# An encoder trunk on one core: the first strips fetched in another order, squares summed on GpSimd, and eight idle products in a LayerNorm

## The chip, the cores and the metric

The kernel runs on one core of a Trainium2 chip. A core has five engines that run side by side and meet at semaphores: TensorE (products; the profile's PE, and PEld for its weight loads), VectorE (DVE), ScalarE (ACT), GpSimd (POOL) and SyncE (SP), whose queue issues nearly all the transfers here. TensorE writes its results to PSUM; operands lie in SBUF. The metric is the device time of one execution in microseconds, as the median of several runs. Beside the runs there is one profiled execution, and its trace is what is read here.

## The reference

Two layers over 512 tokens of width 1024, all in float32. Each sub-layer is `x = x + RMSNorm(f(RMSNorm(x)))`.

```python
for i in range(DEPTH):                      # DEPTH = 2
    g = sandwich_gains[i]
    h = rms_norm(x, g[0])
    m = parallel_conv_mla(h, ...) if i % 2 == 0 else conformer_conv(h, ...)
    x = x + rms_norm(m, g[1])
    h = rms_norm(x, g[2])
    x = x + rms_norm(squared_relu_mlp(h, mlp_w1[i], mlp_w2[i]), g[3])

def conformer_conv(h, w_pw1, b_pw1, w_dw, b_dw, ln_g, ln_b, w_pw2, b_pw2):
    u = h @ w_pw1 + b_pw1
    a, g = jnp.split(u, 2, axis=-1)
    u = depthwise_conv(a * jax.nn.sigmoid(g), w_dw) + b_dw
    u = jax.nn.silu(layer_norm(u, ln_g, ln_b))
    return u @ w_pw2 + b_pw2
```

Layer 0 has a short gated convolution and eight heads of latent attention with one input projection (`w_in`); layer 1 has the Conformer module above. Each layer ends with an MLP of hidden width 4096.

## The kernel before

**Layout.** Activations lie with channels on the 128 partitions and tokens along the free axis: eight tiles of 128 channels (`NC` = 8). A float32 product is made as three products of rounded parts. Every operand is split into a high half (`hi`, the value rounded to the product's input type) and a low half (`lo`, the rest); `mm` (L239) issues high by high (L243), high weight by low activation (L244), low weight by high activation (L245).

**Strips.** Weights come in strips of 128 output columns, 128x1024 elements, 512 KB. `strip` (L207) issues the DMA into `raw` (two buffers at the start), lets ScalarE write `whi` (L220) and GpSimd write `wlo = raw - whi` (L221). With `cuts` it does this in pieces of columns, each piece with a DMA, an ACT and a POOL instruction. A strip's column piece k is the weight for channel tile k.

**The start.** Inside a block with the order of TensorE, VectorE and ScalarE written out by hand (L574), products go through `bit(i, k)` (L584): strip i of the input projection with channel tile k of x, three products of 512 columns (L590 to L592). `busy(n)` (L578) issues n products with a tile of zeros that nobody reads. `scale_x(j)` (L598) fetches x tile j, multiplies it by the gain on VectorE (L601) and writes its high half on ScalarE (L602); `rest_x(j)` (L605) writes the low half on VectorE (L607). `square_x` and `add_x` (L611, L615) make the sum of squares for the first RMSNorm, whose sum over channels is a product with a column of ones (L365, in `Sum.done`). Strips 0 and 1 are walked through side by side, then strip 2, then strip 3. The order of SP's and GpSimd's instructions is left to a planner that simulates the program when it is built.

**Two halves.** From the first layer's output projection on, the tokens are worked in halves A and B, so that one half's products cover the other's norms. The list `M2` names the steps of the last phase in order: `up`, `down` (MLP), `pw1`, `pw2` (Conformer), `join` (residual and next norm), `norm` (the LayerNorm). A `join` or `norm` is a chain that TensorE can't feed itself; while it is written out, `pace` and `hold` (L300, L307) pull the other half's next steps in, as many as stand in the list before this half's next one. In `M2` only VectorE's order is the written one; TensorE's, ScalarE's, GpSimd's and SP's are the planner's.

**The sums.** `Sum.square` (L345) squares a tile on ScalarE (L355) into PSUM and puts the addition on a list, which VectorE does at the next `settle` (L330); `done` sums over channels on TensorE (L365); `rstd` (L381) is a chain of twelve small VectorE instructions (L388 to L416); `spread` (L426) puts the result on all partitions with two or three small products (L430). `rstds` (L374) is these three in a row. `layer_norm` (L900) of a half subtracts the mean (L914), sums the squares, multiplies by the root (L922), applies gain, bias and silu (L925) and splits the result into `h` (L227, L230), which `pw2` reads.

**The gain row.** `gtok` holds the last norm's gain on all partitions, for the end of half B, where tokens lie on the partitions. It has a place of its own from the beginning, and its DMA is written at L1030, in the first `turn` step near the end.

Of the kernel before, what the change touches and what calls it, by code (L numbers as in the profile page):

```python
# [9 lines left out]
F32 = mybir.dt.float32  # L10
# [6 lines left out]
P = 128  # L17
T = 512
# [109 lines left out]
def trunk(ctx: ExitStack, tc: tile.TileContext, a, out: bass.AP, out_b: bass.AP):  # L128
# [23 lines left out]
    def tmp(kind, dt=F32):  # L152
        if kind in CHAIN:
            return new(ap, kind, CHAIN[kind], HW, dt)
        tag, bufs, w = scope["tags"][kind]
        return new(scope["sb"], tag, bufs, w, dt)
# [35 lines left out]

    kst = cp.tile([P, NK], F32, name="kst")
    vec = cp.tile([P, NV], F32, name="vec")
    gtok = cp.tile([P, D], F32, name="gtok")
    ident = kst[:, K_ID : K_ID + P]
    sel = kst[:, K_SEL : K_SEL + P]
    one = kst[:, K_ONE : K_ONE + 1]
# [5 lines left out]
        nc.sync.dma_start(t.t, a["xT"][j * P : (j + 1) * P, :])  # L204


    def strip(src, cuts=()):  # L207
        n = src.shape[-1]
        scope["raws"] += 1
        more = scope["tags"].get("raw")  # L210
        if more and scope["raws"] > RAW0[scope["name"]] and scope["raws"] % (N_RAW + more[1]) < more[1]:
            raw = tmp("raw")[:, :n]
        else:
            raw = new(wp, "raw", N_RAW, STRIP)[:, :n]
        hi = new(wp, "whi", N_W, STRIP, F32R)[:, :n]
        lo = new(wp, "wlo", N_W, STRIP, F32R)[:, :n]
        for c0, c1 in zip((0, *cuts), (*cuts, n)):
            r, h = raw[:, c0:c1], hi[:, c0:c1]
            nc.sync.dma_start(r, src[:, c0:c1])
            nc.scalar.activation(h, r, AF.Copy)  # L220
            nc.gpsimd.tensor_tensor(out=lo[:, c0:c1], in0=r, in1=h.bitcast(F32), op=ALU.subtract)  # L221
        return hi, lo
# [91 lines left out]
    class Sum:  # L314

        def __init__(self, n, seg, eng=None, whole=False):
            self.n, self.seg, self.eng, self.whole = n, seg, eng or scope["sum"], whole
            self.parts, self.i, self.n_sq, self.own = [], 0, 0, False  # L320

# [23 lines left out]
        def square(self, src, spare=None):  # L345


            first = self.n_sq == 0 and self.n > 1
            self.n_sq += 1
            last = self.n_sq == self.n and not self.whole  # L350
            if first or last:
                t = tmp(("acc1" if first else "sq") + ("" if self.seg.w <= HW else "f"))[:, : self.seg.w]
            else:
                t = scratch(self.seg.w) if spare is None else spare
            nc.scalar.activation(t, src, AF.Square)  # L355
            late.append(lambda: self.add(t, first))
# [14 lines left out]
                    )  # L371
            return s

    def rstds(total, ratio=None):  # L374

        hold()
        r = rstd(total.done(), D, ratio)
        hold()
        return spread(r, total.seg)

# [75 lines left out]
    def join(xs, ms, s, post, pre, hs, seg, h, mlp):  # L456

        hv = hs
        bc = rstds(s, lack.pop(h, None))

        t, ssq = {}, Sum(NC, seg, whole=WHOLE[0])
        for j in range(NC + 3):
            if j < NC:
                t[j] = scratch(seg.w)
                nc.vector.tensor_tensor(out=t[j], in0=ms[j][seg.sl], in1=bc, op=ALU.mult)
            i = j - 1
            if 0 <= i < NC:  # L470
                nc.vector.scalar_tensor_tensor(
                    out=t[i], in0=t[i], scalar=col(post + i), in1=xs[i][seg.sl], op0=ALU.mult, op1=ALU.add
                )
                nc.scalar.activation(xs[i][seg.sl], t[i], AF.Copy)
                if not mlp:
                    settle()
                    ssq.square(t[i], t[i])
            i = j - 2
            if mlp and 0 <= i < NC:
                nc.vector.scalar_tensor_tensor(  # L480
                    out=t[i], in0=t[i], scalar=col(pre + i), in1=R0[:, seg.sl], op0=ALU.mult, op1=ALU.mult
                )
                nc.scalar.activation(hv[i][0][seg.sl], t[i], AF.Copy)
            i = j - 3
            if mlp and 0 <= i < NC:
                nc.vector.tensor_tensor(
                    out=hv[i][1][seg.sl], in0=t[i], in1=hv[i][0][seg.sl].bitcast(F32), op=ALU.subtract
                )
            pace(4 if mlp else 3)
        if mlp:  # L490
            for j in range(NC):
                ssq.square(xs[j][seg.sl])
                settle(1)
                pace(1)
            hold()
            lack[h] = ratios(h, seg, ssq)
            return
        bc = rstds(ssq)
        nc.scalar.activation(table(), ssq.parts[0][:, :1], AF.Sigmoid)
        for j in range(NC):  # L500
            t = scratch(seg.w)
            nc.vector.scalar_tensor_tensor(
                out=t, in0=xs[j][seg.sl], scalar=col(pre + j), in1=bc, op0=ALU.mult, op1=ALU.mult
            )
            settle()
            split((hv[j][0][seg.sl], hv[j][1][seg.sl]), t, nc.vector, late=late)
            pace(2)
        settle()
# [65 lines left out]
    with tc.manual_schedule(engines={E.PE, E.DVE, E.Activation}):  # L574
# [3 lines left out]
        def busy(n):  # L578
            for _ in range(n):
                nc.tensor.matmul(bank, idle[:, :P], idle, start=True, stop=True)  # L580
# [14 lines left out]
        win, scaled, sq = [], [], {}  # L595
        total = ps("o")

        def scale_x(j):  # L598
            load_x(xs[j], j)
            t = misc()  # L600
            nc.vector.tensor_scalar(out=t, in0=xs[j].t, scalar1=col(gains(0, 0) + j), scalar2=None, op0=ALU.mult)  # L601
            nc.scalar.activation(hs[j][0].t[:, :T], t, AF.Copy)  # L602
            scaled.append(t)

        def rest_x(j):  # L605
            hi, lo = (h.t[:, :T] for h in hs[j])
            nc.vector.tensor_tensor(out=lo, in0=scaled[j], in1=hi.bitcast(F32), op=ALU.subtract)  # L607
# [7 lines left out]
            nc.vector.tensor_tensor(out=dst, in0=total, in1=sq[j], op=ALU.add)  # L615
            return dst

        scale_x(0)
        win.append(strip(a["win"][0], cuts=(128,)))
        rest_x(0)  # L620
        bit(0, 0)
        busy(10)
        scale_x(1)
        win.append(strip(a["win"][1], cuts=(256, 512, 768)))
        bit(1, 0)
        for j in range(2, NC + 1):
            if j < NC:
                scale_x(j)
            if j >= 5:
                square_x(j - 5)  # L630
            rest_x(j - 1)
            bit(0, j - 1)
            bit(1, j - 1)
        win.append(strip(a["win"][2]))
        nc.sync.dma_start(kst, a["consts"])
        nc.sync.dma_start(vec[:, V_QN:], a["vecs"][:, V_QN:])
        for j in range(1, NC):
# [262 lines left out]
    def layer_norm(seg):  # L900
# [7 lines left out]
        hold()  # L908
        total = spread(mu, seg)
        nc.scalar.activation(table(), mu[:, :1], AF.Silu)  # L910
        s2 = Sum(NC, seg, whole=WHOLE[2])
        for c in range(NC):
            v = vs[c][:, seg.sl]
            nc.vector.tensor_tensor(out=v, in0=v, in1=total, op=ALU.add)  # L914
            settle()
            s2.square(v)
            pace(2)
        rb = rstds(s2)
        hold()
        for c in range(NC):  # L920
            v = vs[c][:, seg.sl]
# [235 lines left out]
    def run(program, in_order=True):  # L1157
# [66 lines left out]
    ph = phase(  # L1224
        "m2",
        acc=["S", "pj", "S", "pj", "S"],
        u=("u", NC, UW), hid=("hid", 2 * NC, HW), y=("y", 3, HW), sg=("y", 3, HW),
        raw=("raw2", RAWS["m2"], STRIP),
    )
    us.extend(tmp("u") for _ in range(NC))  # L1230
    vs = [m.t for m in ms]
    run(M2)
    ph.__exit__(None, None, None)
# [109 lines left out]
```

## Time and profile before

| | |
|---|---|
| median of 3 runs | 1163.99 us (1163.5 to 1165.43) |
| profiled execution | 1163.42 us, span in the trace 1161.6 us |
| TensorE busy | 1137.3 us, 98% of the span, 8514 products |
| GpSimd busy | 849.5 us, 73%, 802.6 of it in L221 |
| ScalarE, VectorE busy | 661.7 us (57%), 644.6 us (55%) |
| first L365 (end of the start on TensorE) | at 28.45 us |
| LayerNorm of half A | first L914 at 631.00 us, first product of `pw2` at 647.14 us |

Times are in microseconds from the start of the span, the mean of one instruction in ns where a view groups them. A row of the order of time has start, duration, engine, line, operation, output and inputs; in brackets stands how long the engine had been idle and what released it. Products are pipelined: a row's duration is longer than the step from one to the next. A row `L365 ... x4` holds records of the same line one behind the other.

### The profile page before, as it was taken

The numbers are of one execution on the slowest core, as the hardware profiler recorded it, in microseconds if no ns is written. First come the engines' busy times: TensorE is split into PE (matmuls) and PEld (weight loads), VectorE is DVE, ScalarE is ACT, GpSimd is POOL, SyncE is SP. The second block draws the span as 40 slices with busy tenths as digits, with TensorE's granted clock in tenths as the row PEclk, the third lists the DMA queues.
The fourth block names the chain that finished last, engine by engine and source line by source line (L and its number), as shares of the span: only waits on it lengthen the run. The fifth ranks groups of instructions, "written<-read, shape, count | busy, mean of one in ns | idle before, by whom it ended". The sixth has DMA issues, their size and how long they took to land.

```text
span 1161.6 us, 22196 instructions
## 1 busy us (share of the span) xinstructions
PE 1137.3 (98%) x8514; PEld 1084.6 (93%) x8514; DVE 644.6 (55%) x1684; ACT 661.7 (57%) x1212; POOL 849.5 (73%) x409
## 2 busy tenths in 40 slices
PE   8999999999999999999999899999999999999997
PEld 6888778999999999999999899999999999898896
DVE  5762698464522122669996355589995354131124
ACT  5531686466744455744656776755555777455451
POOL 4684574149878778688898588789788778788880
PEclk9999999999999999999999899999999999999999
DMA  6431331036555555555565365556555455475531
GB/s 205 138 126 30 107 113 60 1 113 236 188 165 187 172 180 176 170 164 182 182 217 184 128 199 184 180 176 206 168 196 182 164 174 187 160 242 173 174 126 37
DMA packets 55114, 184.48 MB, mean 159 GB/s; under 512 B 6368, under 2 KB 10080, under 8 KB 55008
## 3 DMA queue, kind: packets, MB, share of 16 engines
q1 hardware_dynamic: 54576, 182.41, 47.8%
q8 instruction: 67, 1.10, 0.4%
q10 hardware_dynamic: 432, 0.66, 0.2%
q14 instruction: 39, 0.32, 0.1%
HBM read 180.94 MB, written 2.10 MB: 158 GB/s over the span
## 4 chain that ended last, share of the span: by engine, by line
PE 92%; ACT 2%; DMA 2%; DVE 2%; issue 1%; POOL 1%; SPq 0%; DVEq 0%; ACTq 0%; POOLq 0%
PE S L243 21%; PE S L244 21%; PE S L245 21%; PE pj L243 5%; PE pj L244 5%; PE pj L245 5%; PE S L1048 4%; PE pj L1048 4%; POOL wlo L221 1%; PE mi L828 1%; DMA raw<-in_win 1%; PE mi L365 1%; ACT whi L220 1%; PE mi L430 1%; PE o L244 1%
## 5 line engine op out<-in xcount | busy, mean ns | idle before, releaser
L221 POOL TENSOR_TENSOR wlo<-raw,whi 128x1024 fp32r<-128x1024 f32 (+2 forms) x347 | 802.6, 2330 | 257.0 <-ACT whi L220 255.3
L220 ACT ACTIVATE whi<-raw 128x1024 fp32r<-128x1024 f32 (+2 forms) x347 | 356.5, 1033 | 364.1 <-PE S L244 162.9
L243 PE MATMUL S<-h,whi 128*128 128x256 f32 (+3 forms) x1200 | 343.7, 290 | 4.9 <-ACT h L227 3.0
L244 PE MATMUL S<-h,whi 128*128 128x256 f32 (+3 forms) x1200 | 345.6, 289 | 0.0
L245 PE MATMUL S<-h,wlo 128*128 128x256 f32 (+3 forms) x1200 | 345.4, 289 | 0.0
L243 PEld LDWEIGHTS S<-h,whi 128*128 128x128 f32 x1200 | 227.0, 191 | 9.1 <-ACT h L227 3.4
L244 PEld LDWEIGHTS S<-h,whi 128*128 128x128 f32 x1200 | 228.5, 190 | 3.0
L245 PEld LDWEIGHTS S<-h,wlo 128*128 128x128 f32 x1200 | 228.5, 190 | 2.8
L890 DVE SCALAR_TENSOR_TENSOR pj<-u,taps,pj 128x256 f32<-128x256 f32 x464 | 193.0, 485 | 1.4
L243 PE MATMUL S<-hid,whi 128*128 128x256 f32 (+2 forms) x672 | 187.8, 281 | 2.0 <-DVE acc L330 2.0
L245 PE MATMUL S<-hid,wlo 128*128 128x256 f32 (+2 forms) x672 | 188.7, 282 | 0.0
L244 PE MATMUL S<-hid,whi 128*128 128x256 f32 (+2 forms) x672 | 188.6, 281 | 0.0
L243 PEld LDWEIGHTS S<-hid,whi 128*128 128x128 f32 x672 | 126.5, 189 | 3.0 <-DVE acc L330 2.6
L245 PEld LDWEIGHTS S<-hid,wlo 128*128 128x128 f32 x672 | 127.1, 189 | 0.0
L244 PEld LDWEIGHTS S<-hid,whi 128*128 128x128 f32 x672 | 126.8, 189 | 0.0
L243 PE MATMUL pj<-h,whi 128*128 128x256 f32 (+3 forms) x320 | 95.6, 299 | 0.3 <-DVE h L230 0.3
L244 PE MATMUL pj<-h,whi 128*128 128x256 f32 (+3 forms) x320 | 95.7, 299 | 0.0
L245 PE MATMUL pj<-h,wlo 128*128 128x256 f32 (+3 forms) x320 | 95.5, 298 | 0.0
L233 DVE TENSOR_TENSOR hid<-S,hid 128x256 fp32r<-128x256 f32 (+2 forms) x103 | 43.3, 421 | 50.9 <-ACT hid L227 50.5
L243 PEld LDWEIGHTS pj<-h,whi 128*128 128x128 f32 x320 | 60.9, 190 | 2.1 <-DVE h L230 0.6
L245 PEld LDWEIGHTS pj<-h,wlo 128*128 128x128 f32 x320 | 60.9, 190 | 1.8 <-issue 0.2
L244 PEld LDWEIGHTS pj<-h,whi 128*128 128x128 f32 x320 | 60.9, 190 | 1.8 <-issue 0.2
(298 smaller groups left out, 1795.4 us busy)
## 6 DMA issues: line engine op xcount, KB each, us to landing
raw<-in_w SPq DMA_DIRECT2D x224, 512.0 KB, 3.3
raw<-in_pw SPq DMA_DIRECT2D x48, 512.0 KB, 3.3
raw<-in_w2t SPq DMA_DIRECT2D x32, 512.0 KB, 3.3
raw<-in_win SPq DMA_DIRECT2D x16, 512.0 KB, 3.3
x<-in_xT SPq DMA_DIRECT2D x16, 256.0 KB, 4.5
raw<-in_wout SPq DMA_DIRECT2D x8, 512.0 KB, 3.4
raw<-in_wq SPq DMA_DIRECT2D x8, 192.0 KB, 2.4
out<-x SPq DMA_DIRECT2D x8, 128.0 KB, 3.2
```

What stands on the lines that cost most here:

```text
L220: nc.scalar.activation(h, r, AF.Copy)
L221: nc.gpsimd.tensor_tensor(out=lo[:, c0:c1], in0=r, in1=h.bitcast(F32), op=ALU.subtract)
L233: eng.tensor_tensor(out=lo, in0=src, in1=hi.bitcast(F32), op=ALU.subtract)
L243: nc.tensor.matmul(acc, sh, mh, start=i == 0, stop=False)
L244: nc.tensor.matmul(acc, sh, ml, start=False, stop=False)
L245: nc.tensor.matmul(acc, sl, mh, start=False, stop=i == n - 1)
L365: nc.tensor.matmul(s[:, b : b + 1], q[:, sl.start - self.seg.lo : sl.stop - self.seg.lo], one, start=i == 0, stop=i == len(self.parts) - 1,)
L430: nc.tensor.matmul(o[:, sl], r[:, b : b + 1].to_broadcast([bw, P]), ident[:bw, :bw], start=True, stop=True,)
L828: nc.tensor.transpose(tp[:, kb * P : (kb + 1) * P], pr_[:, kb * P : (kb + 1) * P], ident)
L890: nc.vector.scalar_tensor_tensor(out=dst, in0=src, scalar=wk, in1=acc, op0=ALU.mult, op1=ALU.add)
L1048: nc.tensor.matmul(acc, x, w, start=start, stop=stop)
```

## The change

Four things, in one edit:

1. **Order of fetching.** `scale_x` is taken apart: `fetch_x` has the DMA and the scaling, the rest stays. x tile 1 is fetched behind the first piece of strip 0 and ahead of its other pieces, of which there are now three; that first piece is split ahead of x tile 0's high half. Six idle products in place of ten; the products of strip 0 with tile 1 come ahead of those of strip 1 with tile 0; strip 2 is fetched and split ahead of x tile 6's scaling, where it had been behind all of strips 0 and 1.
2. **Gain row.** `gtok` gets its place in the last phase, in memory used for other things before, and not from the beginning.
3. **Squares on GpSimd.** In the joins that don't lead to an MLP and in the LayerNorms, ScalarE writes the squares to SBUF, and the additions of the second to the seventh go to GpSimd. The first is the sum's own tile, the eighth is still added on VectorE.
4. **Eight products.** In the LayerNorm of half A, behind L365 of the sum of squares, eight products of the sum's tile with the identity go to a PSUM bank of the kind `S`, which nobody reads.

```diff
-    gtok = cp.tile([P, D], F32, name="gtok")
...
-    def strip(src, cuts=()):
+    def strip(src, cuts=(), between={}):
...
         for c0, c1 in zip((0, *cuts), (*cuts, n)):
+            between.get(c0, lambda: None)()
...
+            if self.pool and self.n_sq < self.n:
+
+                t = tmp("acc1" if first else "sq")[:, : self.seg.w]
+                nc.scalar.activation(t, src, AF.Square)
+                if first:
+                    self.parts, self.i = [t], 1
+                else:
+                    self.i += 1
+                    acc = self.parts[0]
+                    nc.gpsimd.tensor_tensor(out=acc, in0=acc, in1=t, op=ALU.add)
+                self.own = True
+                return
...
+        def idle(self, n):
+
+            o = ps("S")[:, :P]
+            for _ in range(n):
+                nc.tensor.matmul(o, self.parts[0][:, :P], ident, start=True, stop=True)
+
+    def rstds(total, ratio=None, idle=0):
 
         hold()
-        r = rstd(total.done(), D, ratio)
+        s = total.done()
+        if idle:
+            total.idle(idle)
+        r = rstd(s, D, ratio)
         hold()
         return spread(r, total.seg)
...
-        t, ssq = {}, Sum(NC, seg, whole=WHOLE[0])
+        t, ssq = {}, Sum(NC, seg, whole=WHOLE[0], pool=not mlp)
...
-        def scale_x(j):
+        def fetch_x(j):
             load_x(xs[j], j)
             t = misc()
             nc.vector.tensor_scalar(out=t, in0=xs[j].t, scalar1=col(gains(0, 0) + j), scalar2=None, op0=ALU.mult)
-            nc.scalar.activation(hs[j][0].t[:, :T], t, AF.Copy)
             scaled.append(t)
+
+        def scale_x(j):
+            if len(scaled) == j:
+                fetch_x(j)
+            nc.scalar.activation(hs[j][0].t[:, :T], scaled[j], AF.Copy)
...
-        scale_x(0)
-        win.append(strip(a["win"][0], cuts=(128,)))
-        rest_x(0)
+        fetch_x(0)
+
+        def second():
+            scale_x(0)
+            rest_x(0)
+            scale_x(1)
+
+        win.append(strip(a["win"][0], cuts=(128, 384, 640), between={128: second}))
         bit(0, 0)
-        busy(10)
-        scale_x(1)
+        busy(6)
+        scale_x(2)
+        rest_x(1)
+        bit(0, 1)
         win.append(strip(a["win"][1], cuts=(256, 512, 768)))
         bit(1, 0)
-        for j in range(2, NC + 1):
+        bit(1, 1)
+        for j in range(3, NC + 1):
+            if j == 6:
+                win.append(strip(a["win"][2]))
             if j < NC:
                 scale_x(j)
             if j >= 5:
...
-        win.append(strip(a["win"][2]))
...
-        s2 = Sum(NC, seg, whole=WHOLE[2])
+        s2 = Sum(NC, seg, whole=WHOLE[2], pool=True)
...
-        rb = rstds(s2)
+        rb = rstds(s2, idle=8 if seg is A2 else 0)
...
-        u=("u", NC, UW), hid=("hid", 2 * NC, HW), y=("y", 3, HW), sg=("y", 3, HW),
+        u=("u", NC, UW), gtok=("gtok", 1, D), hid=("hid", 2 * NC, HW), y=("y", 3, HW), sg=("y", 3, HW),
...
     us.extend(tmp("u") for _ in range(NC))
+    gtok = tmp("gtok")
```

More of the change, by code (lines that the diff above doesn't have):

```diff
@@ L314, in trunk, with __init__ @@
     class Sum:
-        def __init__(self, n, seg, eng=None, whole=False):
+        def __init__(self, n, seg, eng=None, whole=False, pool=False):
+            self.pool = pool
             self.n, self.seg, self.eng, self.whole = n, seg, eng or scope["sum"], whole
@@ L372, in done @@
             return s
-    def rstds(total, ratio=None):
+        def idle(self, n):
[3 more added lines that the diff above has]
+    def rstds(total, ratio=None, idle=0):
         hold()
-        r = rstd(total.done(), D, ratio)
+        s = total.done()
+        if idle:
+            total.idle(idle)
+        r = rstd(s, D, ratio)
         hold()
```

## The prediction

> **What bounds the kernel now.** I read the page first, then the order of time in the first 30 us, then the same view around the first half's LayerNorm, last the clock by stretches.
>
> ```profile
> span 1161.6 us, 22196 instructions
> PE 1137.3 (98%) x8514; PEld 1084.6 (93%) x8514; DVE 644.6 (55%) x1684; ACT 661.7 (57%) x1212; POOL 849.5 (73%) x409
> ```
>
> TensorE has work for all but 24.3 us of 1161.6. So only what moves TensorE counts: a place where it stands still, a place where its clock is low, or products added to it. Two places can answer to this change, the start and the LayerNorm of half A. In the order of time (start, duration, engine, line; in brackets the idle time before it and its releaser) the start reads:
>
> ```profile
> 4.88 0.60 ACT L602 ACTIVATE h<-mi 128x512 fp32r<-128x512 f32 x1 [2.66 <-DVE mi L601]
> ...
> 5.51 0.69 DVE L607 TENSOR_TENSOR h<-mi,h 128x512 fp32r<-128x512 f32 x1 [0.66 <-ACT h L602]
> ...
> 7.15 2.45 PE L580 MATMUL S<-tq 128*128 128x512 f32 x10
> 7.91 4.88 POOL L221 TENSOR_TENSOR wlo<-raw,whi 128x896 fp32r<-128x896 f32 x5 [1.70 <-ACT whi L220]
> 7.96 0.75 DVE L601 TENSOR_SCALAR mi<-x,vec 128x512 f32<-128x512 f32 x1 [1.75 <-DMA x<-in_xT]
> ...
> 9.24 1.32 ACT L220 ACTIVATE whi<-raw 128x256 fp32r<-128x256 f32 x4
> ...
> 10.76 0.51 PE L591 MATMUL S<-h,wlo 128*128 128x512 f32 x1 [0.56 <-POOL wlo L221]
> ...
> 12.74 0.39 PE L590 MATMUL pj<-h,whi 128*128 128x512 f32 x1
> ...
> 15.59 0.60 ACT L611 ACTIVATE o<-x 128x512 f32<-128x512 f32 x1
> ...
> 16.47 0.60 ACT L602 ACTIVATE h<-mi 128x512 fp32r<-128x512 f32 x1 [0.29 <-DVE mi L601]
> ...
> 19.39 1.05 ACT L220 ACTIVATE whi<-raw 128x1024 fp32r<-128x1024 f32 x1
> ...
> 20.51 2.38 POOL L221 TENSOR_TENSOR wlo<-raw,whi 128x1024 fp32r<-128x1024 f32 x1 [7.72 <-ACT whi L220]
> ...
> 20.97 0.39 PE L590 MATMUL pj<-h,whi 128*128 128x512 f32 x1
> ...
> 22.94 0.50 PE L591 MATMUL pj<-h,wlo 128*128 128x512 f32 x1 [1.58 <-POOL wlo L221]
> ...
> 23.90 0.69 DVE L615 TENSOR_TENSOR ycat<-o,ycat 128x512 f32<-128x512 f32 x1
> ```
>
> Up to 10.76 TensorE marks time: ten idle products, then a wait for GpSimd, which splits the rest of strip 0 in one piece (from 7.91) before strip 1's first piece. From 12.74, the first product of column tile 2, to 20.97 it runs without a gap: six tiles with six products each in 8.23 us, 1.37 a tile and 0.23 a product. The row of 20.97 is the first product of strip 2; the second waits until 22.94 for the low half of that strip. ScalarE reached that strip only at 19.39 though its data had landed at 14.7, as a piece of the chain of waits says (issued 10.05, 4.66 long); the other piece here, the sum for the norm, is where the start ends for TensorE:
>
> ```profile
> 10.05 4.66 DMA raw<-in_win
> ...
> 28.45 1.23 PE mi L365 x12
> ```
>
> **Part 1, the start.** *The second stall.* Between 20.97 and 22.94 lie 1.97 us in place of one product's 0.23: 1.74 us are lost. With strip 2's split ahead of column tile 6, ScalarE comes to it once the data are there (14.7, or 14.9 if the buffer comes free 0.2 us later) and once the square of 15.59 is done, on a schedule some 0.4 earlier at 15.8. Then 1.05 on ScalarE to 16.8 and 2.38 on GpSimd, idle there for 7.72 us, to 19.2, ahead of the new 20.4. The price is ScalarE's 1.05 us in a stretch with little room: tile 6's high half ends at 17.4 (before: 16.47 + 0.60 = 17.1), and its products come at 12.74 + 4 x 1.37 - 0.6 = 17.6. So the 1.74 us are gained whole; with a late landing up to 1 us of it is lost again.
>
> *The first stall.* The chain that decides it now is: the low half of tile 0 ends at 6.20 (5.51 + 0.69); then, with x tile 1 fetched ahead of the rest of strip 0, its scaling (0.75) to 6.95, its high half on ScalarE (0.60) to 7.6, then strip 0's second piece there (0.33 from the four of 9.24) to 7.9. The earlier landing of that tile (before: 7.96) is worth nothing beyond 6.20, where VectorE comes free. GpSimd's pieces cost:
>
> ```profile
> L221 POOL TENSOR_TENSOR wlo<-raw,whi 128x256 fp32r<-128x256 f32 x8 | 5.8, 733 | 7.4 <-ACT whi L220 7.4
> L221 POOL TENSOR_TENSOR wlo<-raw,whi 128x384 fp32r<-128x384 f32 x8 | 8.4, 1047 | 15.8 <-ACT whi L220 15.8
> L221 POOL TENSOR_TENSOR wlo<-raw,whi 128x1024 fp32r<-128x1024 f32 x329 | 785.9, 2407 | 226.8 <-ACT whi L220 225.1 <-DMA raw<-in_w 0.5 <-PE S L245 0.5
> ```
>
> In a run five pieces took 4.88, so a 256-wide one goes by in 0.69 and the 384-wide one in 0.95: 7.9 + 0.69 + 0.69 + 0.95 = 10.2, and strip 1's first piece at 10.9. That is 0.14 later than 10.76, but by then the three products of strip 0 and tile 1 (0.68, half of 1.37) are done in what was idle time. Tile 2's products start at 12.74 + 0.14 - 0.68 = 12.2, 0.5 to 0.6 earlier; I take 0.6. Four idle products less (0.98 of the 2.45) lie in that same wait and count nothing by themselves. If strip 1's piece comes 0.7 later, nothing is gained here; if GpSimd takes it ahead of strip 0's last piece, 1.5.
>
> VectorE needs 0.75 + 0.69 per tile, within 0.05 us of TensorE's beat, so it follows; the sum of squares ends at 24.6 (23.90 + 0.69), ahead of the new 26.1, where L365 falls. **Start: -0.6 - 1.74 = -2.3 us**, bounds -3.2 and -0.7.
>
> **Part 2, gain row moved.** Its row among the DMA issues (size, us to landing), and three rows of the list of all TensorE's waits (total, times, longest), the last two being all its waits for split strips:
>
> ```profile
> gtok<-in_gain SPq DMA_DIRECT2D x1, 512.0 KB, 5.6
> ```
>
> ```profile
> PE S L243 <- ACT h L227: 3.0, 2, 1.9
> ...
> PE pj L591 <- POOL wlo L221: 1.6, 1, 1.6
> ...
> PE S L591 <- POOL wlo L221: 0.6, 1, 0.6
> ```
>
> The 512 KB go from the start to the last phase, on the same SP queue, where nothing waits for them until the kernel's last products. The strips queued behind them have a lead: after the start TensorE waits for none. I price it at 0; without that lead it would be 5.6 us once.
>
> **Part 3, squares on GpSimd.** In two joins and two LayerNorms six additions each move from VectorE to GpSimd; the eighth square is still added on VectorE. Around the LayerNorm of half A:
>
> ```profile
> 630.36 0.61 PE L430 MATMUL mi<-kst,s 128*128 128x128 f32 x4
> 630.72 0.36 PE L243 MATMUL S<-hid,whi 128*128 128x240 f32 x1
> ...
> 633.13 0.42 DVE L330 TENSOR_TENSOR acc<-acc,o 128x256 f32<-128x256 f32 x1 [1.04 <-ACT o L355]
> ...
> 638.37 0.42 DVE L330 TENSOR_TENSOR acc<-acc,mi 128x256 f32<-128x256 f32 x1 [0.63 <-ACT mi L355]
> ...
> 641.33 0.50 PE L365 MATMUL mi<-kst,acc 128*128 128x1 f32 x4
> ...
> 642.55 0.28 PE L245 MATMUL S<-h,wlo 128*128 128x240 f32 x1
> ...
> 644.14 1.06 PE L430 MATMUL mi<-kst,s 128*128 128x128 f32 x4 [1.31 <-DVE s L416]
> ...
> 644.96 0.41 DVE L233 TENSOR_TENSOR hid<-S,hid 128x240 fp32r<-128x240 f32 x1 [0.55 <-ACT hid L227]
> 645.28 1.07 DVE L922 TENSOR_TENSOR m<-m,mi 128x256 f32<-128x256 f32 x3
> ...
> 652.30 0.42 DVE L230 TENSOR_TENSOR h<-mi,h 128x256 fp32r<-128x256 f32 x1 [0.45 <-ACT h L227]
> ...
> 653.20 0.28 PE L243 MATMUL pj<-h,whi 128*128 128x256 f32 x1
> ```
>
> The last addition ended at 638.8, but its product on TensorE stands behind others until 641.33: 2.5 us of slack. An addition of 256 columns on GpSimd is bounded by 0.73 (the 256-wide split, also two operands) against 0.42 on VectorE; six make 4.4 us. GpSimd is full of splits of 2.4 us there, so each batch of ready additions waits for one. Two batches of three cost 2 x (2.4 + 2.2) = 9.2 us from the second square (633.1), so 642.3, and 0.4 for the last one on VectorE: some 1.3 us after 641.33. All six in one gap end inside the slack, and where VectorE, rid of its waits for each square, lets the sum come earlier and TensorE's order follows, up to 2.5 us are won. Bounds +1.3 and -2.5. I take 0, the case inside the slack: TensorE's order, and not the chain, set 641.33. The splits that wait in turn hold up nobody as long as TensorE does not come to wait for strips, and part 2 shows that it did not. The joins and LayerNorm B go with this: beside LayerNorm A's 1.9 us only 1.1 of waiting for h is left to win in all of them, and none of them can lose before its own slack is used up.
>
> **Part 4, the eight products.** Each is a product of a 128x128 tile with the 128x128 identity in full precision, as L430's two are (four records in the row of 630.36, two for each product). Those let the next product go 0.36 us after they began: 0.18 each, 8 x 0.18 = 1.4 us. They find a gap of 1.31 (before 644.14). If they stand ahead of the eight products that end at 642.55, the B half's split (645.37) and with it L922 come some 0.5 us later; if behind, nothing is late. What they can bring is the clock, in the view by stretches:
>
> ```profile
> 641.00:642.80 1.80, 1.80 (x17) 1.64 (x15) 0.80 (x6) 0.75 (x2) 1.80 (x1) 1.00 0.68 223
> ...
> 644.50:647.10 2.60, 0.71 (x4) 0.41 (x2) 1.40 (x4) 1.77 (x6) 1.79 (x1) 0.50 0.53 186
> 647.10:651.20 4.10, 4.06 (x19) 4.06 (x20) 3.76 (x11) 4.04 (x11) 0.00 (x0) 0.50 0.39 128
> ```
>
> The granted clock (the column ahead of the last two) is 0.50 from 644.5 to 651.2. That looks like 3.3 us, but the products there follow h, whose last low half is ready at 652.72, and the group ends at 653.20. At full clock two products of 0.12 (256 columns, half of 0.23) remain after 652.72, so 652.96: the clock costs 0.24 us. Bounds -0.24 and +0.5; I take -0.1, since the products fit the gap to within 0.1 us.
>
> [...]
>
> **Sum.** -2.3 + 0 + 0 - 0.1 = -2.4 us. The profiled execution took 1163.42 (1.8 around its span), so 1161.0; the median of the runs is 1163.99, 0.57 above it, so 1161.6.
>
> **Rivals.** *The sum of squares takes back half:* two batches, +1.3 in LayerNorm A: 1162.9. For it GpSimd's 1.80 busy of 1.80 us from 641.0; against it the 2.5 us of slack. *Slower:* GpSimd puts one split of 2.4 us ahead of each of the six additions in LayerNorm A: 6 x (2.4 + 0.73) = 18.8 from 633.1, plus 0.4, is 652.3, 11.0 after 641.33, less 2.4: +8.6, 1172.6 as a median. It turns to a loss once that chain ends 2.4 us past 641.33. Against it: additions that are ready together follow one another. [...] *The start does not give it:* strip 2 lands late and holds tile 6 back, strip 1's piece is late: -0.7, 1163.3. *More than asked:* the sum is ready earlier and TensorE's order follows, -2.5 more in LayerNorm A: 1159.1.
>
> **Numbers.** Forecast 0.43, half taken back 0.17, slower 0.16, start fails 0.12, more 0.12. What can be told from no change is 0.2%, 2.3 us; the forecast lies on that edge, so of its own part some 0.33 is faster. Faster 0.33 + 0.12 = 0.45, slower 0.16, the same 0.39. The likeliest's own range is 1160.5 to 1162.5; with the cases beside it 1159.0 to 1164.8, which leaves out most of the slower one.
>
> **What would show it.** Right: L365 of the start near 26.1, no wait before L591 of strip 2, the wait near 11 still there; L365 of LayerNorm A with no wait on GpSimd; eight products ahead of L430 and clock 1.00 throughout; pw2's first group still paced by h. Wrong: splits between the additions with TensorE idle after the B half has run out, or a clock below 1.00 in the first 25 us.

## The result, and the profile after

The changed kernel takes 1189.2 us (median of 4 runs, 1188.13 to 1190.42) against 1163.86 us before: a ratio of 1.0218, 95% interval 1.0206 to 1.023. It is 25 us slower. The forecast was 1161.6, and its range ended at 1164.8. The head of the page of the profile after:

```profile
span 1187.3 us, 22208 instructions
...
PE 1147.1 (97%) x8526; PEld 1093.8 (92%) x8526; DVE 636.5 (54%) x1660; ACT 661.1 (56%) x1214; POOL 867.4 (73%) x435
```

TensorE is busy 9.8 us more and the span is 25.7 us longer, so 16 us of the loss are new standing time. In the rest lie products at a granted clock of 0.50 (646.60 to 651.00, below) and products that nobody reads; it was not taken apart. VectorE has 24 instructions fewer, GpSimd 26 more: the 24 additions and two more pieces of strip 0. (L220 to L245 keep their numbers; L330 is now L331, L355 is L354 or L368, L365 is L378, L430 is L452, L580 is L602, L590 to L592 are L612 to L614, L867 is L902, L922 is L957; L360 is the addition on GpSimd, L391 the eight products.)

**The start.** The changed kernel in order of time on TensorE (start, duration, engine, line; in brackets the idle time before it):

```profile
11.05 0.50 PE L613 MATMUL S<-h,wlo 128*128 128x512 f32 x1 [0.31 <-POOL wlo L221]
...
12.31 0.39 PE L612 MATMUL pj<-h,whi 128*128 128x512 f32 x1
...
25.92 1.39 PE L378 MATMUL mi<-kst,ycat 128*128 128x1 f32 x12
```

The row of 25.92 stood at 28.29 before: 2.37 us gained. The wait near 11 is still there, the one before strip 2's second product is gone.

**Where it is lost.** The same view of both kernels, at waits before the same products in both, which serve as milestones. Before:

```profile
473.64 0.35 PE L243 MATMUL S<-h,whi 128*128 128x240 f32 x1 [0.30 <-ACT pj L355]
...
487.28 0.65 PE L243 MATMUL S<-h,whi 128*128 128x272 f32 x3 [1.03 <-ACT h L227]
...
647.14 1.01 PE L243 MATMUL S<-h,whi 128*128 128x256 f32 x3 [1.93 <-ACT h L227]
...
700.70 0.38 PE L243 MATMUL S<-hid,whi 128*128 128x240 f32 x1 [0.76 <-DVE acc L330]
...
760.05 0.38 PE L243 MATMUL S<-h,whi 128*128 128x240 f32 x1 [0.82 <-DVE u L867]
...
957.00 0.39 PE L243 MATMUL S<-hid,whi 128*128 128x256 f32 x1 [0.68 <-DVE acc L330]
```

After:

```profile
471.94 0.38 PE L243 MATMUL S<-h,whi 128*128 128x240 f32 x1 [0.42 <-DVE hid L233]
...
488.86 0.64 PE L243 MATMUL S<-h,whi 128*128 128x272 f32 x3 [1.03 <-ACT h L227]
...
662.05 0.62 PE L243 MATMUL S<-h,whi 128*128 128x256 f32 x3 [4.26 <-ACT h L227]
...
715.45 0.38 PE L243 MATMUL S<-hid,whi 128*128 128x240 f32 x1 [0.76 <-DVE acc L331]
...
776.66 0.38 PE L243 MATMUL S<-h,whi 128*128 128x240 f32 x1 [0.82 <-DVE u L902]
...
982.58 0.38 PE L243 MATMUL S<-hid,whi 128*128 128x256 f32 x1 [0.66 <-DVE acc L331]
```

Each difference of two milestones is what has been gained or lost up to there, and its steps name the places:

| stretch | after minus before at its end | lost in it |
|---|---|---|
| start and attention | -1.70 | -1.70 |
| join of half A | +1.58 | 3.28 |
| LayerNorm of half A, up to pw2's first product | +14.91 | 13.33 |
| pw2 | +14.75 | -0.16 |
| join of half B | +16.61 | 1.86 |
| LayerNorm of half B | +25.58 | 8.97 |
| the rest (spans 1161.6 and 1187.3) | +25.7 | 0.1 |

So the loss is in the four places where squares are now added on GpSimd, and in no other. The largest, on TensorE in the changed kernel (631.96 is the mean's L452, 630.36 before):

```profile
631.96 0.61 PE L452 MATMUL mi<-kst,s 128*128 128x128 f32 x4
...
646.58 0.98 PE L378 MATMUL mi<-kst,acc 128*128 128x1 f32 x4 [7.95 <-DVE acc L331]
647.42 3.76 PE L391 MATMUL S<-kst,acc 128*128 128x128 f32 x16
650.83 0.55 PE L243 MATMUL S<-h,whi 128*128 128x240 f32 x1
...
654.49 0.61 PE L452 MATMUL mi<-kst,s 128*128 128x128 f32 x4
```

GpSimd in the same stretch, and then three rows of VectorE:

```profile
634.51 2.40 POOL L221 TENSOR_TENSOR wlo<-raw,whi 128x1024 fp32r<-128x1024 f32 x1 [0.21 <-ACT whi L220]
636.87 0.73 POOL L360 TENSOR_TENSOR acc<-acc,sq 128x256 f32<-128x256 f32 x1
637.56 2.36 POOL L221 TENSOR_TENSOR wlo<-raw,whi 128x1024 fp32r<-128x1024 f32 x1
639.88 0.71 POOL L360 TENSOR_TENSOR acc<-acc,sq 128x256 f32<-128x256 f32 x1
640.56 2.33 POOL L221 TENSOR_TENSOR wlo<-raw,whi 128x1024 fp32r<-128x1024 f32 x1
642.86 3.12 POOL L360 TENSOR_TENSOR acc<-acc,sq 128x256 f32<-128x256 f32 x4
```

```profile
646.01 0.42 DVE L331 TENSOR_TENSOR acc<-acc,o 128x256 f32<-128x256 f32 x1 [9.30 <-POOL acc L360]
...
659.86 0.41 DVE L233 TENSOR_TENSOR hid<-S,hid 128x240 fp32r<-128x240 f32 x1 [2.72 <-ACT hid L227]
660.19 1.08 DVE L957 TENSOR_TENSOR m<-m,mi 128x256 f32<-128x256 f32 x3
```

The sum is whole at 646.43, 14.47 us after the mean's product; before it took 8.43 (638.79 less 630.36). Counted from the mean's product, the 13.3 us come in three pieces. The sum's product L378 comes 14.62 us after it in place of 10.97: 3.65. From there to the root's L452 it is 7.91 in place of 2.81, 5.10 more: the eight products (647.42 to 650.83, 3.41 us), then 24 products of half B's up-projection, which were in front of the sum before. From L452 to pw2's first product it is 7.56 in place of 3.00, 4.56 more: another 24 such products, whose split (L233, 659.86) stands ahead of the LayerNorm's multiplications (L957, 660.19) on VectorE. The clock in the stretch of the eight products (columns as in the prediction):

```profile
646.60:651.00 4.40, 4.40 (x21) 4.40 (x22) 2.03 (x13) 0.00 (x0) 0.00 (x0) 0.50 0.00 0
```

The eight products meant to keep TensorE's clock came behind a gap of 7.95 us and ran at 0.50 themselves.

**The other three places.** The list of TensorE's waits after has a row that the kernel before does not have (total, times, longest):

```profile
PE mi L378 <- DVE acc L331: 17.0, 4, 8.0
```

These are the products of the four sums: TensorE stands 1.68 us for them in join A, 7.95 in LayerNorm A, 0.78 in join B and 6.56 in LayerNorm B. In the last, the mean's product and the sum's, before and then after:

```profile
885.93 0.61 PE L430 MATMUL mi<-kst,s 128*128 128x128 f32 x4
896.34 0.50 PE L365 MATMUL mi<-kst,acc 128*128 128x1 f32 x4
```

```profile
902.26 0.61 PE L452 MATMUL mi<-kst,s 128*128 128x128 f32 x4
919.20 0.98 PE L378 MATMUL mi<-kst,acc 128*128 128x1 f32 x4 [6.56 <-DVE acc L331]
```

The sum's product comes 16.94 us after the mean's in place of 10.41. The 24 products between it and the root's product then take 5.26 us in place of 2.95, at a granted clock of 0.50 (919.20 to 924.70) in place of 1.00 (896.30 to 899.50). In both joins and in this LayerNorm GpSimd does one addition, one split, up to the fifth addition, and the sixth follows the fifth.

### The profile page after: what moved, and what is told of

Its sections match the earlier page's. It is cut to its first block, busy times and chain, and to the rows that moved or that the text cites. A ratio compares the mean times of both kernels' runs of the same rounds, so it can differ in the third digit from the quotient of the medians.

```text
span 1187.3 us, 22208 instructions
## 1 busy us (share of the span) xinstructions
PE 1147.1 (97%) x8526; PEld 1093.8 (92%) x8526; DVE 636.5 (54%) x1660; ACT 661.1 (56%) x1214; POOL 867.4 (73%) x435
## 5 line engine op out<-in xcount | busy, mean ns | idle before, releaser
L221 POOL TENSOR_TENSOR wlo<-raw,whi 128x1024 fp32r<-128x1024 f32 (+3 forms) x349 | 804.4, 2322 | 264.8 <-ACT whi L220 263.9
L220 ACT ACTIVATE whi<-raw 128x1024 fp32r<-128x1024 f32 (+3 forms) x349 | 356.1, 1027 | 383.0 <-PE S L244 184.7
L245 PE MATMUL S<-h,wlo 128*128 128x256 f32 (+3 forms) x1200 | 346.5, 290 | 0.0
L245 PEld LDWEIGHTS S<-h,wlo 128*128 128x128 f32 x1200 | 230.3, 192 | 2.8
L245 PE MATMUL S<-hid,wlo 128*128 128x256 f32 (+2 forms) x672 | 189.0, 282 | 0.0
L245 PEld LDWEIGHTS S<-hid,wlo 128*128 128x128 f32 x672 | 127.8, 190 | 0.0
L245 PE MATMUL pj<-h,wlo 128*128 128x256 f32 (+3 forms) x320 | 95.6, 299 | 0.0
L233 DVE TENSOR_TENSOR hid<-S,hid 128x256 fp32r<-128x256 f32 (+2 forms) x103 | 43.3, 421 | 63.2 <-ACT hid L227 62.8
L245 PEld LDWEIGHTS pj<-h,wlo 128*128 128x128 f32 x320 | 60.9, 190 | 1.8 <-issue 0.2
```

Of the source, the lines that this page charges most:

```text
L233: eng.tensor_tensor(out=lo, in0=src, in1=hi.bitcast(F32), op=ALU.subtract)
L245: nc.tensor.matmul(acc, sl, mh, start=False, stop=i == n - 1)
```

## The experiments

Three theories of the loss. **Theory 1:** the additions stand between splits of 2.4 us on GpSimd, in an order that is fixed before the run, so the sums are late. **Theory 2:** the eight products. **Theory 3:** the squares now share three buffers in SBUF, and ScalarE waits for them. The time in each run's LayerNorm of half A is read as the distance from the mean's L452 to pw2's first product: 16.78 before, 30.09 after.

### The fetch order and the gain row alone

```diff
-        t, ssq = {}, Sum(NC, seg, whole=WHOLE[0], pool=not mlp)
+        t, ssq = {}, Sum(NC, seg, whole=WHOLE[0], pool=False)
...
-        s2 = Sum(NC, seg, whole=WHOLE[2], pool=True)
+        s2 = Sum(NC, seg, whole=WHOLE[2], pool=False)
...
-        rb = rstds(s2, idle=8 if seg is A2 else 0)
+        rb = rstds(s2, idle=0)
```

> The changed kernel with all additions of squares back on VectorE and without the eight products; the new order of fetching and the moved gain row stay. Every theory of the loss puts it elsewhere, so this run prices the start and the gain row alone: the first sum's product (L378) near 25.9 us in place of 28.29 (-2.37), of which the trace of the changed kernel keeps 1.7 to 1.8 by 222 us. Expected: 1161.7 to 1162.2 as a median, 0.15% to 0.2% below the kernel before. If the moved gain row, queued among the last phase's strips, costs anything, the time comes back to 1164 or above.

> The fetch order and the moved gain row alone once more, on the same chip as the sixteen products. The first run gave a ratio of 0.9983 to the kernel before. Expected 0.998 to 0.999 again; at 1.000 the start's gain would be lost on the way.

Measured: 1161.6 us, ratio 0.9983 (0.9973 to 0.9994); the second time 1161.56 us, 0.9989 (0.998 to 0.9997). In the second run's trace L378 of the start stands at 25.81, half A's LayerNorm takes 16.79, and late milestones keep the lead:

```profile
758.30 0.38 PE L243 MATMUL S<-h,whi 128*128 128x240 f32 x1 [0.83 <-DVE u L902]
```

That is 1.75 us ahead of 760.05, and the span, 1159.8, is 1.8 ahead of 1161.6. The gain row's transfer was issued at 256.3 us there and at 11.4 in the kernel before; the first milestone, at 471.13, is still 2.51 us ahead, so the transfer shows no cost at its new place. What its absence from the start is worth was not tried by itself. This part of the change is a small gain, 1.7 to 2.2 us in the medians, and the whole loss of 25 us (27.6 against this run) lies in the other two parts. It is the fastest version that was run.

### Without the eight products

```diff
-        rb = rstds(s2, idle=8 if seg is A2 else 0)
+        rb = rstds(s2, idle=0)
```

> The changed kernel without the eight products alone. Theory 1 (additions that alternate with 2.4 us splits on GpSimd make the sums late, the products only add their own 3.4 us at half clock): 1189.2 - 3.4 = 1185.8, with the wait of about 8 us before L378 of half A's LayerNorm still there. Theory 2 (the eight products, put ahead of ready products of the other half and in the same buffer, are the main cost): 1175 or below.

Measured: 1185.48 us, ratio 1.0185 (1.0171 to 1.0199), 3.7 us less than with them. Theory 1 had 1185.8, from the 3.4 us of the products alone. In the profiled executions the LayerNorm of half A gives back 4.5 us and join A, where the granted clock was 1.00 in place of 0.51 behind the gap, another 1.6 (last section). GpSimd and TensorE in this LayerNorm of half A:

```profile
635.14 0.73 POOL L360 TENSOR_TENSOR acc<-acc,sq 128x256 f32<-128x256 f32 x1
635.84 2.41 POOL L221 TENSOR_TENSOR wlo<-raw,whi 128x1024 fp32r<-128x1024 f32 x1
638.22 0.72 POOL L360 TENSOR_TENSOR acc<-acc,sq 128x256 f32<-128x256 f32 x1
...
647.25 1.51 POOL L360 TENSOR_TENSOR acc<-acc,sq 128x256 f32<-128x256 f32 x2
```

```profile
649.37 0.98 PE L378 MATMUL mi<-kst,acc 128*128 128x1 f32 x4 [7.11 <-DVE acc L331]
```

Six additions, a split ahead of each of the first five, 3.0 to 3.1 us from one to the next. Here the 48 up products of half B do run ahead of the sum, TensorE still stands 7.11 us, and the LayerNorm takes 25.62: 8.84 us lost by the additions alone.

### The eight products alone, in bank S

Additions on VectorE, as in the first experiment's first two edits; the eight products stay.

> The changed kernel with the additions back on VectorE; the eight products stay. Theory 1: as the fetch order alone, 1161.7 to 1162.2, or up to 1.4 more if the products at full clock lie on the path (to 1163.6). Theory 2: 1165 or more, with half A's LayerNorm still losing most of its 13.3 us.

Measured: 1168.24 us, ratio 1.0035 (1.0023 to 1.0047), 6.6 us above the fetch order alone. Theory 1's number was wrong, and so was the part of theory 2 that gave the products most of the 13.3: the LayerNorm takes 22.79, a loss of 6.0. In this trace L378 has moved to the front of the up products, waits 1.91 us for the sum, the granted clock is 0.61 from 638.40 to 642.00, the eight products take 3.1 us (638.89 to 642.00), and all 48 up products follow them. So the loss in this LayerNorm has two causes of about like size, 8.8 and 6.0 alone and 13.3 together.

### The eight products in another bank, and sixteen of them

```diff
-            o = ps("S")[:, :P]
+            o = ps("o")[:, :P]
```

and in a second kernel `idle=16` in place of 8; additions on VectorE in both.

> Additions on VectorE, the eight products kept, but written into bank o in place of bank S; nothing else differs from the run that keeps the products in S. Theory 2a (the products cost little by themselves; they took a turn of the three S buffers, which the up-projection of half B uses too, so its 48 products had to follow them and no longer covered the sum and the root): those products are back in front of L378, and the time is that of the fetch order alone, 1161.6, plus 0 to 1. Theory 2b (the products cost their own time on the path, at half clock): it stays at 1166 to 1168.

> As the run with the products in bank o, with sixteen of them in place of eight. In that run eight took 1.78 us (640.14 to 641.92) ahead of the last eight up products of half B, whose split on VectorE (L233 at 645.19) stands in front of the LayerNorm's own multiplications (L957 at 645.51); pw2's first product came 1.8 us later, counted from L452 of the mean. If the products cost what they delay that split by: 1.8 us more, 1165.2 to 1165.7. If their cost is only that they find no gap and break the order once: no more than the run with eight, 1163.7. If they win something back by the clock: below 1163.

Measured: 1163.68 us with eight, ratio 1.0005 (0.9996 to 1.0014); 1167.15 with sixteen, 1.0028 (1.0017 to 1.0038). With eight, 40 of the up products are back in front of the sum; the LayerNorm takes 18.57. On TensorE:

```profile
640.14 2.03 PE L391 MATMUL o<-kst,acc 128*128 128x128 f32 x16
641.92 0.36 PE L244 MATMUL S<-h,whi 128*128 128x240 f32 x1
```

So of the 6.0 us, 4.2 came from the bank: the products took a turn of bank S, which has three buffers and holds the up-projection's results, and the order made the up products follow. The other 1.8 is their own time, 1.78 us from 640.14 to 641.92, 0.22 each: they delay the last eight up products, and the split L233 of those (645.19) stands on VectorE ahead of L957 (645.51). Sixteen bring the LayerNorm to 20.36, again 1.79 more, as expected; the median moved by 3.5 where 1.5 to 2.0 was expected, and in that profiled execution the start had kept only 0.4 us of its gain. Theory 2b (1166 to 1168) falls. Theory 2a had the mechanism, but its 0 to 1 us above the fetch order alone was too little: eight products cost about 2 us more than none, and the hope of a gain by the clock falls too.

### Squares in SBUF, added on VectorE

```diff
-                    nc.gpsimd.tensor_tensor(out=acc, in0=acc, in1=t, op=ALU.add)
+                    late.append(lambda: nc.vector.tensor_tensor(out=acc, in0=acc, in1=t, op=ALU.add))
```

> The changed kernel with the squares still written to its three buffers, but the additions on VectorE; the eight products stay. Theory 1 (the additions' place on GpSimd): near 1162 to 1163.6, L378 of half A's LayerNorm without a long wait. Theory 3 (three buffers in place of six hold ScalarE and so the sum back, on whatever engine adds): half A's LayerNorm stays late by several us, 1175 or more.

Measured: 1185.69 us, ratio 1.0192 (1.0178 to 1.0206). Theory 1's number was wrong by 22 us or more. Theory 3's condition held (1175 or more), but its cause does not show: ScalarE's longest waits ahead of these squares are for VectorE's subtraction of the mean (2.50 and 2.66 us), not for a buffer. The LayerNorm of half A takes 29.24 us, against 22.79 with squares in PSUM and the same eight products in S. The trace points to a third. VectorE, then GpSimd:

```profile
635.88 2.41 DVE L360 TENSOR_TENSOR acc<-acc,sq 128x256 f32<-128x256 f32 x1 [1.08 <-ACT sq L354]
...
638.54 0.41 DVE L360 TENSOR_TENSOR acc<-acc,sq 128x256 f32<-128x256 f32 x1
...
640.48 2.25 DVE L360 TENSOR_TENSOR acc<-acc,sq 128x256 f32<-128x256 f32 x1 [0.21 <-ACT sq L354]
```

```profile
635.61 2.40 POOL L221 TENSOR_TENSOR wlo<-raw,whi 128x1024 fp32r<-128x1024 f32 x1 [0.21 <-ACT whi L220]
640.10 4.83 POOL L221 TENSOR_TENSOR wlo<-raw,whi 128x1024 fp32r<-128x1024 f32 x2 [2.09 <-ACT whi L220]
```

An addition of the same size on VectorE took 0.41 us while GpSimd was idle (638.54) and 2.41 and 2.25 us where it started during a split (635.88, 640.48); the first of these ended 0.28 us after its split did (638.29 against 638.01). Grouped by what they read (duration in ns: least, median, most):

```profile
L331 DVE TENSOR_TENSOR acc<-acc,pj x29: 388/422/441, 226.4 to 988.6; 128x256 f32<-128x256 f32 x14, 128x272 f32<-128x272 f32 x9, 128x240 f32<-128x240 f32 x6
L360 DVE TENSOR_TENSOR acc<-acc,sq x24: 393/1096/2615, 466.2 to 915.3; 128x256 f32<-128x256 f32 x12, 128x272 f32<-128x272 f32 x6, 128x240 f32<-128x240 f32 x6
```

In this trace no addition with one operand in PSUM (pj) took over 0.44 us, and of those with both in SBUF half took over 1.09. In the second run of the fetch order alone, additions with one operand in PSUM ran at 0.41 to 0.42 us beside splits that filled GpSimd from 630.36 to 635.31, and so they did in the kernel before beside those from 632.91 to 637.86. So with the squares in SBUF the additions meet the splits on either engine: on GpSimd in its queue, on VectorE by lasting until a split that runs has ended. What holds VectorE there was not shown.

### Five buffers for the squares

```diff
-CHAIN = {"sq": 3, "acc1": 2, "t2": 1}
+CHAIN = {"sq": 5, "acc1": 2, "t2": 1}
```

> The changed kernel with five buffers for the squares in place of three; the order on GpSimd is the same. Theory 1 (the additions wait for splits in GpSimd's order): 1189 within 1.5. Theory 3 (ScalarE waits for a free buffer, up to 2.56 us in the trace, and so the sum is late): 1180 or below.

Measured: 1189.8 us, ratio 1.0229 (1.0209 to 1.0249). Five squares then run in a row on ScalarE (634.97, 1.63 us) and are ready at 636.60, ahead of the first addition; GpSimd's additions still come at the same distances as in the changed kernel (637.52, 640.54, and four from 643.52), with a split between. So theory 3 is out, and additions that are ready together do not follow one another in this order.

### Two batches of three

Without the eight products, and with GpSimd's instructions of this phase in the order in which the program writes them.

```diff
-        order = tc.manual_schedule(engines={mybir.EngineType.DVE}) if in_order else nullcontext()
+        order = tc.manual_schedule(engines={mybir.EngineType.DVE, mybir.EngineType.Pool} if scope["name"] == "m2" else {mybir.EngineType.DVE}) if in_order else nullcontext()
```

> All additions on GpSimd, no eight products, and GpSimd's order in this phase as written instead of planned: in each LayerNorm two batches of three additions with one split between them, in place of one split between nearly all; in each join batches of one, two, two and one. Theory 1 (each split ahead of an addition costs 2.4 us of the sum): the sum of half A's LayerNorm ends near 642.7 in place of 649.4, the loss there falls from 8.8 to about 2 us, that of half B's likewise from 9.0 to about 2, the joins by a part of 5: some 1170, in place of 1185.5. If the price is the additions' own time on GpSimd or the squares' buffers: 1183 or more. If splits held up behind waiting additions make strips late, TensorE waits for low halves (L245) and the time is above 1172.

Measured: 1177.14 us, ratio 1.012 (1.0106 to 1.0133): 8.3 us less than with the planned order, not the 15 that theory 1 gave. In half A's LayerNorm GpSimd does this:

```profile
639.08 2.38 POOL L360 TENSOR_TENSOR acc<-acc,sq 128x256 f32<-128x256 f32 x3 [9.94 <-ACT sq L354]
641.42 2.40 POOL L221 TENSOR_TENSOR wlo<-raw,whi 128x1024 fp32r<-128x1024 f32 x1
643.77 2.39 POOL L360 TENSOR_TENSOR acc<-acc,sq 128x256 f32<-128x256 f32 x3
```

L378 there no longer waits, and the LayerNorm takes 18.04: 1.26 us lost in place of 8.84. Half B's LayerNorm, from the mean's product (898.49) to the milestone that stood at 957.00 (971.98), loses 2.4 in place of 9.3. So in the two LayerNorms the splits between the additions are the cause. The joins did not gain: from trace to trace, A loses 3.6 us and B 4.5. There the other half of the same conflict shows. With its order as written GpSimd stands before the additions with splits behind them (9.94 us in this LayerNorm), and the list of TensorE's waits has a row that neither kernel had in this phase; five of its six waits lie in the joins:

```profile
PE S L245 <- POOL wlo L221: 4.1, 6, 1.0
```

### The joins alone

Additions on GpSimd in the joins; LayerNorms on VectorE, no eight products (the second and third edit of the first experiment).

> Additions on GpSimd in the two joins alone, both LayerNorms on VectorE, no eight products. The trace of the changed kernel puts 3.3 us on join A and 1.9 on join B. If these losses belong to the joins: 1161.6 + 5.2 = 1166.8. If they only follow from what is late elsewhere: 1161.6 to 1162.5.

Measured: 1168.65 us, ratio 1.0045 (1.0032 to 1.0059). By the milestones join A costs 3.28 us (473.41 to 490.33, against 473.64 to 487.28) and join B 1.87, as in the changed kernel, and the LayerNorm of half A is back at 16.78. The losses belong to the joins. The median is 1.9 us above the sum of 1166.8; in the profiled execution 1.6 us were lost at 166 to 172, a stretch of which the last section tells. About half of join A's 3.28 us goes with products that come 0.21 us apart in place of 0.11 (484.94 to 488.34); the kernel without the eight products, with a granted clock of 1.00 there, did not have this loss, and the last section shows it in the changed kernel at 0.51.

### Ten idle products at the start

The fetch order alone, with one more edit:

```diff
-        busy(6)
+        busy(10)
```

> The fetch order and the moved gain row alone, with the ten idle products of the kernel before at the start in place of six. In three of the eleven profiled executions of the new fetch order TensorE stood 1.2 to 2.0 us in all between 8 and 12 us, the granted clock there fell to 0.65 to 0.72, and the first sum's product came only 0.2 to 0.8 us earlier than before in place of 2.0 to 2.5. If the four idle products that were taken out kept the clock: L378 at 25.8 to 26.0, clock 1.00 up to 26 us, and the lower edge of the runs unchanged, the median 1160.8 to 1161.6. If they stand in the way of the products of tile 2 (0.98 us for four): L378 up to 1 us later and the median 1162 or more.

Measured: 1162.57 us, ratio 0.9995 (0.9986 to 1.0004). The clock is 1.00 up to 26 us, but L378 stands at 26.43, against 25.81 with six: the four products stand in the way for about half a microsecond, and the median is 1 us higher. Six look better, but the intervals of the ratios overlap.

## Why the prediction failed

**Part 1** was right. Forecast -2.3 with L365 near 26.1; measured -2.37 at 25.92, the second stall gone, the first still there, tile 2 at 12.31 where 12.2 was forecast. About 0.7 of it is given back up to the end of the attention stage, and the medians keep 1.7 to 2.2. One sentence was too strong: that the four idle products less "count nothing by themselves". In three of the eleven profiled executions with six of them the clock between 10 and 14 us was 0.65, 0.68 and 0.72 (the eight products alone in S, the sixteen, the batches) and most of the gain went: the sum's product came only 0.2 to 0.8 us earlier than before. Putting the four back did not lower the median; whether they keep the clock can't be told from one profiled execution.

**Part 2** was right as far as it shows: no cost of the gain row is seen. It was only run together with the new order of fetching.

**Part 3** is the step that failed: "I take 0, the case inside the slack: TensorE's order, and not the chain, set 641.33". The 2.5 us of slack were there, but the chain became 10.5 us longer without the eight products (it ends 18.98 us after the mean's product, 649.22 less 630.24, in place of 8.43) and not at most 4. The sum was built on one addition's 0.73 us, which was right (0.71 to 0.73 measured in this LayerNorm), and on how many splits come between the additions, which was not: two in all, by "additions that are ready together follow one another". In the runs the order without the eight products is one split, one addition, five times over, and then the sixth addition. With two batches of three, the case that the bound +1.3 was worked out from, LayerNorm A loses 1.26, but that they agree is chance. The bound counts a split ahead of each batch and a sum whole 1.3 us after 641.33. In the run only one split lies between the batches, and the sum is whole 10.38 us after the mean's product (646.61 less 636.23), 0.6 ahead of where L365 stood before; 0.9 of the 1.26 is that TensorE's order now puts L378 behind all 48 up products. The premise of batches fails by itself: with five buffers, five squares were ready at once and splits still came between the additions. That order is the planner's; why it chose it was not tried.

The rival "slower" had the mechanism and the place, LayerNorm A. Its price there was 11.0 us, with six splits (the +8.6 is what is left after the 2.4 of the other parts); the additions alone cost 8.84, with five splits. It was given 0.16. That its 1172.6 lies nearer than the forecast to the measured time does not make it right: it too left out the rest, as did the sentence "Two places can answer to this change". "None of them can lose before its own slack is used up" is true, but those slacks were not read: join A loses 3.3, join B 1.9, LayerNorm B 9.0 us. In LayerNorm B the sum's product comes 16.94 us after the mean's in the changed kernel and 10.41 before (919.20 less 902.26, 896.34 less 885.93), and TensorE waits 6.56 us for it: the same late sum as in LayerNorm A, again with a split between the additions.

**Part 4** failed in size and in kind. "8 x 0.18 = 1.4 us" was 1.78 us in bank o, and 3.1 and 3.4 us at a granted clock of 0.61 and 0.50, behind waits of 1.91 and 7.95 us. The sentence "some 0.5 us later" for L922 named the right neighbour, and it is 1.8. What it missed is the bank: in S they put 48 ready products behind themselves, 4.2 us. Together 6.0 us alone and 3.7 on top of the additions, against the -0.1 forecast. What the clock is worth there was not measured by itself; the products did not keep it (0.50 where they ran in the changed kernel). The gap of 1.31 us that they were to fill had moved, to 7.95 us ahead of them.

The sum was -2.3 + 0 + 0 - 0.1. By the runs it is about -2 for the first two parts, +24 for the additions (1185.48 against 1161.6) and +3.7 for the products on top.

## What to carry to other kernels

An operation that is moved to an engine full of long instructions can cost the wait for its turn at each link of the chain that it is part of, and its own duration is then the smaller part: here six additions of 0.7 us, with a split of 2.4 us ahead of each of five, made a sum 10 us later. Count the links and assume one long instruction before each, unless the order on that engine can be read. Putting the additions in batches helped their own chain (half A's LayerNorm went from 25.62 us to 18.04), and the splits held up behind them were then the ones that were late (4.1 us of waits for low halves). And before a product or a buffer is added "for nothing", look whose turn in that bank it takes and which instruction stands behind it on the next engine.

## What the runs showed of the hardware

In the run with the squares in SBUF and their additions on VectorE, an addition took 0.41 us while GpSimd was idle, and 2.41 and 2.25 us where it started during one of GpSimd's splits, while those with one operand in PSUM (pj) took 0.39 to 0.44. That was the price here of moving a square from PSUM to SBUF where VectorE adds it, and it was not in the prediction.

Behind short gaps the granted clock was lower in some places and executions and not in others. In the kernel before it was 0.50 from 644.50 to 647.10, behind a gap of 1.31 us. In join A, TensorE stands 1.68 us ahead of the sum's product in the changed kernel and 1.66 in the one without the eight products, which come much later. Behind that gap, in the first and in the second:

```profile
482.00:485.00 3.00, 3.00 (x16) 3.00 (x16) 1.90 (x12) 2.15 (x3) 1.01 (x1) 0.51 0.04 11
```

```profile
482.00:485.00 3.00, 3.00 (x28) 3.00 (x29) 1.90 (x12) 2.52 (x4) 1.40 (x1) 1.00 0.03 10
```

The same 28 products take 4.73 us in the first, at 0.51 up to 485.00, and 3.22 in the second, at 1.00 (482.27 to 487.00, 482.07 to 485.29), and join A loses 3.28 us in the first and 1.65 in the second. Two profiled executions of one kernel, the fetch order alone, by stretches, the first from its first run and the second from its second:

```profile
166.00:172.00 6.00, 5.18 (x27) 4.65 (x25) 5.44 (x12) 4.27 (x11) 4.27 (x4) 0.72 0.27 89
```

```profile
166.00:172.00 6.00, 5.62 (x35) 5.05 (x36) 5.71 (x13) 4.81 (x10) 4.70 (x5) 1.00 0.56 171
```

Both have the same two waits of 0.80 us for VectorE 1.9 us apart; in the first the clock is 0.72 and 1.6 us are lost. Three others with the new fetch order (the changed kernel, sixteen products, ten idle products at the start) have the two waits too, 0.79 to 0.81 us each, and a clock of 1.00. What decides it was not found.
